# Layer 0: the up projections made ahead of the sweep become plain fp32 products, 50 of them in place of 46

## The chip, the cores and the metric

The kernel runs on one core of one Trainium2 chip, in one launch. The metric is the time of the launch on the device in microseconds (us). Five engines work side by side, each through its own queue of instructions in a fixed order: PE (TensorE, matrix products), DVE (VectorE), ACT (ScalarE), POOL (GpSimd) and SP (SyncE, which here only starts transfers). An instruction waits at the head of its queue until what it reads is there and what it overwrites is free, and everything behind it on that engine waits too.

## The reference

Two layers of a diffusion transformer over 256 latent tokens and 256 context tokens of width 1024. Each layer mixes tokens (a convolution and two kinds of attention), and then a feed-forward with very many small experts follows. Only that last part is touched:

```python
def chunk_step(xc):
    q = (xc @ w_q).reshape(PEER_CHUNK, PEER_HEADS, 2, PEER_D_KEY)
    s = jnp.einsum('chpk,hpnk->chpn', q, sub_keys).astype(jnp.float32)
    top_s, top_i = lax.top_k(s, PEER_TOPK)
    ...
    best_s, best_pos = lax.top_k(cand_s.reshape(PEER_CHUNK, PEER_HEADS, n_cand), PEER_TOPK)
    idx = jnp.take_along_axis(...)
    g = jax.nn.softmax(best_s, axis=-1).astype(xc.dtype)
    act = jax.nn.gelu(jnp.einsum('cd,chkd->chk', xc, jnp.take(u, idx, axis=0)))
    return jnp.einsum('chk,chkd->cd', g * act, jnp.take(v, idx, axis=0))
```

There are 16,384 rows in `u` and in `v`. For each token 8 heads choose 16 rows each by a score; the token's product with a chosen row of `u` goes through gelu and is the weight of the same row of `v`. Layer 0 does this for all 512 tokens (four tiles of 128), layer 1 for the 256 latent ones.

## The kernel before

**Dense and gathered tiles.** In layer 0 three of the four tiles of 128 tokens are treated densely (384 tokens, `nd`): every row of `u` is multiplied with every token, and a matrix of gates (zero for rows that were not chosen) is multiplied in behind the gelu. The fourth tile is treated by gathers: POOL fetches the chosen rows (tiles `gru` and `grv`), and DVE takes the products. The 16,384 rows are cut into 128 blocks of 128, which the code calls `e`; in this text a block is called an expert.

**The up projection of an expert** (`act`, L622 ff.) multiplies a block of `u` (1024 x 128, eight chunks of 128) with the 384 tokens. The operands are split: `hi` is the value rounded to a narrower fp32 (fp32r), `lo` the rest, and each chunk is three products, hi·hi, lo·hi and hi·lo (`mm3`, L118 to L121), so 24 products of 128x384 into the PSUM tile `psu`. The tokens' halves are `h2` (tiles `ahi_m`, `alo_m`). The block of `u` is split for each expert: ACT makes `hi_u` (L97); `lo_u` is made by POOL in four pieces (L104) for the experts that are made ahead, and by DVE in one (L99) for the others. ACT then takes the gelu into `gact` (L632).

**Ahead of the sweep.** 46 experts have their up projection made ahead: the first `GA[0]` = 4 stay in SBUF, the next `SPILL[0]` = 42 are written to DRAM (`spilled`) and read back later (`gback`). This fills PE while the routing goes on: 16 query projections (`psq`, split as above), the choice of the best 16 by DVE (L644 to L648), then for each of the 24 groups of 16 tokens four DVE operations on 128x2048 f16 (`ohA`, `ohB`, `ohC`, L782 to L786), 32 small PE products (`psg`, L792), four ACT copies (`stage`, L794) and one write of 1 MB of gates to DRAM (`gd`).

**The sweep** (`sweep`) goes through all 128 experts: gelu times gate (`gr`, read back from `gd` for eight experts at a time), a split into `whi` and `wlo`, and the down projection, 18 products of 128x512 into the PSUM tiles `acc`. For an expert that was not made ahead, its up projection comes in between. Gathers are started between experts; `ahead` = `GA[l] + SPILL[l]` is in the formula that paces them.

**Order.** The code says what is to be done; a scheduler that keeps its own timeline decides the order on each engine when the program is built, so an edit in one place can move rows elsewhere. Tiles of one tag share buffers: `raw_u` has three, `hi_u` and `lo_u` have two each, `psu` has two.

**Layer 1** has the same structure with 192 tokens, and its up projections are plain fp32 products already (L630): eight matmuls per expert straight from `raw_u` and the unsplit tokens `h2raw`. In the trace each of these stands as two instructions, so 16 per expert.

## Time and profile before

| | before |
|---|---|
| time, median of 3 runs | 2625.38 us (2622.39 to 2629.26) |
| profiled execution, its own time | 2625.23 us |
| span of its trace, first to last instruction | 2623.5 us |
| PE busy | 2490.8 us, 95% of the span |
| DVE / ACT / POOL busy | 1828.0 / 1054.5 / 1048.3 us |
| mean granted TensorE clock | 0.981 |

Busy times of PE count from the start of a product to its modelled end, and products overlap, so a busy PE can still be starting fewer products than it could. The rate at which it starts them is read from the distance between starts in the timeline. All times in the trace are counted from the start of the span.

### The profile page before, as it was taken

The numbers are of one execution on the slowest core, as the hardware profiler recorded it, in microseconds if no ns is written. First come the engines' busy times: TensorE is split into PE (matmuls) and PEld (weight loads), VectorE is DVE, ScalarE is ACT, GpSimd is POOL, SyncE is SP. The second block draws the span as 40 slices with busy tenths as digits, with TensorE's granted clock in tenths as the row PEclk, the third lists the DMA queues.
The fourth block names the chain that finished last, engine by engine and source line by source line (L and its number), as shares of the span: only waits on it lengthen the run. The fifth ranks groups of instructions, "written<-read, shape, count | busy, mean of one in ns | idle before, by whom it ended". The sixth has DMA issues, their size and how long they took to land.

```text
span 2623.5 us, 38317 instructions
## 1 busy us (share of the span) xinstructions
PE 2490.8 (95%) x13837; PEld 2018.2 (77%) x13837; DVE 1828.0 (70%) x3506; ACT 1054.5 (40%) x1710; POOL 1048.3 (40%) x967
## 2 busy tenths in 40 slices
PE   7999999888899999999999998998999999999997
PEld 4755788777798888998999987856997656777774
DVE  1754589999546678887888885474994457666667
ACT  3345633367533333333333334455454333323333
POOL 4713434768542245544445441831500114332222
PEclk9999999999999999999999999998999999999999
DMA  7343364366878889999999992541579879999996
GB/s 270 115 158 123 131 243 150 116 220 256 298 256 286 289 294 360 334 339 325 357 332 343 339 327 77 195 133 40 166 254 352 281 264 339 381 344 363 352 364 221
DMA packets 274223, 681.44 MB, mean 260 GB/s; under 512 B 25024, under 2 KB 129008, under 8 KB 270960
## 3 DMA queue, kind: packets, MB, share of 16 engines
q1 hardware_dynamic: 127040, 423.48, 45.4%
q0 software_dynamic: 55296, 201.35, 20.7%
q10 hardware_dynamic: 91696, 54.15, 7.2%
q8 instruction: 109, 1.79, 0.3%
q14 instruction: 82, 0.67, 0.1%
HBM read 628.63 MB, written 49.44 MB: 258 GB/s over the span
## 4 chain that ended last, share of the span: by engine, by line
PE 63%; DVE 13%; issue 7%; DMA 7%; POOL 3%; ACT 2%; ACTq 0%; DVEq 0%; SPq 0%; POOLq 0%
PE psu L630 11%; PE acc L119 6%; PE acc L120 6%; PE acc L121 6%; PE acc L834 4%; PE psu L121 4%; PE psu L119 4%; PE psu L120 4%; DMA grv<-in_v,eidx 2%; POOL gru L918 2%; DMA gr<-gd 2%; PE psada L221 2%; DVE ohC L786 1%; DVE ohB L783 1%; PE psq L119 1%
## 5 line engine op out<-in xcount | busy, mean ns | idle before, releaser
L120 PE MATMUL acc<-lo_v,whi 128*128 128x512 f32 x1024 | 410.1, 401 | 1.2 <-DVE lo_v L99 1.0
L99 DVE TENSOR_TENSOR lo_v<-raw_v,hi_v 128x1024 fp32r<-128x1024 f32 x256 | 312.0, 1222 | 137.8 <-ACT hi_v L97 137.2
L97 ACT ACTIVATE hi_v<-raw_v 128x1024 fp32r<-128x1024 f32 x256 | 268.7, 1053 | 274.7 <-PE acc L121 232.1
L630 PE MATMUL psu<-h2raw,raw_u 128*128 128x192 f32 x2048 | 365.4, 330 | 11.5 <-DMA raw_u<-in_u 7.7
L121 PE MATMUL acc<-hi_v,wlo 128*128 128x512 f32 x1024 | 373.1, 392 | 0.0
L630 PEld LDWEIGHTS psu<-h2raw,raw_u 128*128 128x128 f32 x2048 | 339.4, 191 | 42.8 <-issue 21.8
L119 PE MATMUL psu<-ahi_m,hi_u 128*128 128x384 f32 x1024 | 348.5, 340 | 10.4 <-ACT gact L632 10.4
L121 PE MATMUL psu<-ahi_m,lo_u 128*128 128x384 f32 x1024 | 349.3, 341 | 4.9 <-DVE lo_u L99 2.9
L119 PE MATMUL acc<-hi_v,whi 128*128 128x512 f32 x1024 | 346.7, 404 | 4.4 <-ACT hi_v L97 3.5
L120 PE MATMUL psu<-alo_m,hi_u 128*128 128x384 f32 x1024 | 348.4, 340 | 0.0
L918 POOL DMA_INDIRECT gru<-in_u_rows,eidx x128 | 184.8, 1444 | 274.6 <-DVE gback L819 142.0
L119 PEld LDWEIGHTS acc<-hi_v,whi 128*128 128x128 f32 x1024 | 184.8, 188 | 105.4 <-ACT gact L632 32.5
L913 DVE SCALAR_TENSOR_TENSOR h2n<-grv,dots,h2n 128x1024 f32<-128x1024 f32 x190 | 242.9, 1279 | 25.0 <-DMA grv<-in_v,eidx 24.0
L104 POOL TENSOR_TENSOR lo_u<-raw_u,hi_u 128x256 fp32r<-128x256 f32 x184 | 209.8, 1172 | 104.7 <-ACT hi_u L97 97.9
L906 DVE SCALAR_TENSOR_TENSOR gru<-gru,h2n 128x1024 f32<-128x1024 f32 x192 | 232.4, 1220 | 25.0 <-DMA gru<-in_u_rows,eidx 23.2
L918 POOL DMA_INDIRECT grv<-in_v,eidx x128 | 171.9, 1343 | 187.0 <-DVE h2n L913 160.7
L918 POOL DMA_INDIRECT gru<-in_u_rows,egl x64 | 91.0, 1422 | 376.8 <-DMA spilled<-gact 125.6
L120 PEld LDWEIGHTS acc<-lo_v,whi 128*128 128x128 f32 x1024 | 192.7, 188 | 55.8 <-DVE lo_v L99 8.2
L121 PEld LDWEIGHTS acc<-hi_v,wlo 128*128 128x128 f32 x1024 | 192.4, 188 | 37.0 <-DVE wlo L824 0.3
L119 PEld LDWEIGHTS psu<-ahi_m,hi_u 128*128 128x128 f32 x1024 | 194.4, 190 | 16.2 <-ACT gact L632 11.7
L121 PEld LDWEIGHTS psu<-ahi_m,lo_u 128*128 128x128 f32 x1024 | 194.4, 190 | 10.2 <-DVE lo_u L99 3.9
L120 PEld LDWEIGHTS psu<-alo_m,hi_u 128*128 128x128 f32 x1024 | 194.6, 190 | 4.1
(286 smaller groups left out, 4468.1 us busy)
## 6 DMA issues: line engine op xcount, KB each, us to landing
raw_u<-in_u SPq DMA_DIRECT2D x256, 512.0 KB, 6.0
raw_v<-in_v SPq DMA_DIRECT2D x256, 512.0 KB, 6.4
ada<-in_ada SPq DMA_DIRECT2D x96, 512.0 KB, 5.6
gd<-stage SPq DMA_DIRECT2D x24, 1024.0 KB, 5.8
gr<-gd ACTq DMA_DIRECT2D x16, 1536.0 KB, 21.5
raw_wq<-in_w_q SPq DMA_DIRECT2D x32, 512.0 KB, 3.7
raw_wout<-in_w_out SPq DMA_DIRECT2D x24, 512.0 KB, 3.5
gd<-stage SPq DMA_DIRECT2D x12, 960.0 KB, 5.0
```

Source lines behind the costliest of these rows:

```text
L97: S.activation(hi, raw, AF.Copy)
L99: V.tensor_tensor(lo, raw, hi.bitcast(F32), ALU.subtract)
L104: hold(lo_eng.tensor_tensor(lo[sl], raw[sl], hi[sl].bitcast(F32), ALU.subtract), after)
L119: return [PE.matmul(o, lhsT=ahi, rhs=bhi, start=first, stop=False), PE.matmul(o, lhsT=ahi, rhs=blo, start=False, stop=False), PE.matmul(o, ...
L120: PE.matmul(o, lhsT=ahi, rhs=blo, start=False, stop=False),
L121: PE.matmul(o, lhsT=alo, rhs=bhi, start=False, stop=last)]
L221: PE.matmul(ps[o:o + 32, :], lhsT=scw[:, c, :], rhs=w[:, q, :], start=c == 0, stop=c == NC - 1)
L630: PE.matmul(ps[:, :nd], lhsT=u[:, c, :], rhs=h2raw[:, c, :nd], start=c == 0, stop=c == NC - 1)
L834: return [PE.matmul(acc[1][0][k * H:(k + 1) * H], lhsT=ga[:, P:P + H], rhs=raw[:, k * 512:(k + 1) * 512], start=e == 0, stop=e == NE - 1) ...
L906: return V.scalar_tensor_tensor(r, r, 1.0, h2n[g], op0=ALU.mult, op1=ALU.mult, accum_out=dots[:, s:s + 1])
L913: return V.scalar_tensor_tensor(h2n[g], r, dots[:, s:s + 1], h2n[g], op0=ALU.mult, op1=ALU.add)
L918: d = G.indirect_dma_start(out=r, out_offset=None, in_=a["v_rows" if k >= ns else "u_rows"], in_offset=bass.IndirectOffsetOnAxis(ap=eidx[g ...
```

## The change

All experts ahead of the sweep in layer 0 are multiplied as layer 1 does it: plain fp32, straight from `raw_u`, with no split of `u`. There are now 50 of them (`SPILL[0]` = 46). The unsplit tokens that this needs are made on POOL as `h2[0] + h2[1]`, one addition of 128x384 per chunk, into a new tile `hr`. The other 78 experts keep the split and DVE's `lo_u`.

```diff
-SPILL = {0: 42, 1: 32}
+SPILL = {0: 46, 1: 32}
...
+        hr = None
+
         def act(e, tag="gact", bufs=GA[l]):
             ps = bank("mm", f"psu{l}_{e}")
-            if first:
+            if first and e >= GA[l] + SPILL[l]:
                 u = piece(a["u"][l, e], TP, "u", f"u{l}_{e}", G if e < GA[l] + SPILL[l] else V)
                 gemm_t(ps[:, :nd], u, h2, slice(0, nd))
             else:
                 u = load(a["u"][l, e], TP, "u", f"u{l}_{e}")
                 for c in range(NC):
-                    PE.matmul(ps[:, :nd], lhsT=u[:, c, :], rhs=h2raw[:, c, :nd], start=c == 0, stop=c == NC - 1)
+                    PE.matmul(ps[:, :nd], lhsT=u[:, c, :], rhs=hr[:, c, :nd], start=c == 0, stop=c == NC - 1)
...
+            hr = rt.tile([P, NC, nd], F32, name=f"hr{l}") if first else h2raw
...
             for h in range(8):
+                if first:
+
+                    G.tensor_tensor(hr[:, h, :], h2[0][:, h, :nd].bitcast(F32), h2[1][:, h, :nd].bitcast(F32), ALU.add)
```

The built programs show where this puts the instructions. On POOL, in the norm ahead of the queries, `alo_m` is the low half of the tokens that the query products read, and `lo_wq` that of their weights. Before:

```order
L196 TENSOR_TENSOR alo_m0_877<-hraw_g010_2590,ahi_m0_876 128x256
L196 TENSOR_TENSOR alo_m0_877<-hraw_g012_2610,ahi_m0_876 128x256
L196 TENSOR_TENSOR alo_m0_877<-hraw_g014_2630,ahi_m0_876 128x256
L196 TENSOR_TENSOR alo_m0_877<-hraw_g016_2650,ahi_m0_876 128x256
L104 TENSOR_TENSOR lo_wq02_2910<-raw_wq02_2907,hi_wq02_2909 128x256 x4
```

And now:

```order
L196 TENSOR_TENSOR alo_m0_877<-hraw_g010_2590,ahi_m0_876 128x256
L657 TENSOR_TENSOR hr0_2673<-ahi_m0_876,alo_m0_877 128x384 x2
L196 TENSOR_TENSOR alo_m0_877<-hraw_g012_2610,ahi_m0_876 128x256
L196 TENSOR_TENSOR alo_m0_877<-hraw_g014_2630,ahi_m0_876 128x256
L657 TENSOR_TENSOR hr0_2673<-ahi_m0_876,alo_m0_877 128x384 x4
L196 TENSOR_TENSOR alo_m0_877<-hraw_g016_2650,ahi_m0_876 128x256
L657 TENSOR_TENSOR hr0_2673<-ahi_m0_876,alo_m0_877 128x384 x2
L104 TENSOR_TENSOR lo_wq02_2682<-raw_wq02_2679,hi_wq02_2681 128x256 x4
```

All eight additions stand between these rows, six of them ahead of the last `alo_m`.

On PE, the place is the start of the sweep: the last up projections ahead of the first `acc`. Before, the first `acc` stands behind expert 38, and experts 39 to 45 follow between the `acc`:

```order
L119 MATMUL psu0_38_7278<-ahi_m0_876,hi_u0_38_7281 128x384
L120 MATMUL psu0_38_7278<-alo_m0_877,hi_u0_38_7281 128x384
L121 MATMUL psu0_38_7278<-ahi_m0_876,lo_u0_38_7282 128x384
L119 MATMUL acc000_7579<-hi_v0_0_7595,whi0_0_7589 128x512
L120 MATMUL acc000_7579<-lo_v0_0_7596,whi0_0_7589 128x512
```

Now all 50 plain products and two split experts (50 and 51) stand ahead of it:

```order
L632 MATMUL psu0_48_6553<-hr0_2673,raw_u0_48_6554 128x384 x8
L632 MATMUL psu0_49_6567<-hr0_2673,raw_u0_49_6568 128x384 x8
...
L119 MATMUL psu0_51_8325<-ahi_m0_876,hi_u0_51_8328 128x384
L120 MATMUL psu0_51_8325<-alo_m0_877,hi_u0_51_8328 128x384
L121 MATMUL psu0_51_8325<-ahi_m0_876,lo_u0_51_8329 128x384
L119 MATMUL acc000_6586<-hi_v0_0_6602,whi0_0_6596 128x512
```

Of the plain products, 32 experts and a half stand ahead of the last `psg` of the routing and 17 and a half behind it; before it was 33 experts and 20 products, and 12 experts.

On ACT, whose queue also starts the reads of `gr` and `gback`, the place is the first read of gates. Before, it stands behind the gelu of expert 34:

```order
L97 ACTIVATE hi_u0_36_7207<-raw_u0_36_7205 128x1024
L632 ACTIVATE gact0_34_7164<-psu0_34_7130 128x384
L97 ACTIVATE hi_u0_37_7244<-raw_u0_37_7242 128x1024
L817 DMA gr0_0_7586<-gd0_2571 128x24x128
L711 DMA gback0_4_7708<-spilled0_6019 128x384
```

Now it stands behind the gelu of the last expert ahead, number 49, and behind two splits that wait for their loads:

```order
L97 ACTIVATE hi_u0_50_8263<-raw_u0_50_8261 128x1024
L634 ACTIVATE gact0_48_6564<-psu0_48_6553 128x384
L97 ACTIVATE hi_u0_51_8328<-raw_u0_51_8326 128x1024
L634 ACTIVATE gact0_49_6578<-psu0_49_6567 128x384
L823 DMA gr0_0_6593<-gd0_2571 128x24x128
L717 DMA gback0_4_6715<-spilled0_5936 128x384
```

## Rows read from the trace of the kernel before

**Rows 1.** The profile page, its first part: busy us of each engine, its share of the span and its instructions.

```profile
PE 2490.8 (95%) x13837; PEld 2018.2 (77%) x13837; DVE 1828.0 (70%) x3506; ACT 1054.5 (40%) x1710; POOL 1048.3 (40%) x967
```

**Rows 2.** Busy time by stretch: the stretch, its length, then for each engine its busy us and (x) its instructions, the granted clock, the DMA share and GB/s. The first stretch goes from the first `psu` of layer 0 to the first `acc` of the sweep, the next two are its parts up to the last `psg` and behind it, the fourth is the sweep up to its last `acc`, the last a piece of the sweep.

```profile
446.45:715.90 269.45, 224.72 (x1730) 211.17 (x1726) 230.24 (x318) 156.39 (x197) 186.32 (x153) 0.96 0.61 217
446.45:684.60 238.15, 201.05 (x1611) 188.70 (x1608) 227.72 (x314) 145.73 (x183) 174.60 (x136) 0.96 0.57 203
684.60:715.90 31.30, 23.67 (x121) 22.47 (x120) 2.52 (x5) 10.66 (x15) 11.72 (x17) 0.89 0.98 324
715.90:1621.40 905.50, 901.07 (x4441) 803.16 (x4441) 684.86 (x857) 320.07 (x443) 377.11 (x284) 1.00 0.88 308
1000.00:1400.00 400.00, 397.43 (x2010) 360.63 (x2009) 330.02 (x418) 141.37 (x193) 192.55 (x144) 1.00 0.96 339
```

**Rows 3.** The same stretches, PE's instructions on `psu` alone: busy us, (x) products, clock, DMA.

```profile
446.45:715.90 269.45, 181.75 (x936) 0.96 0.61 217
715.90:1621.40 905.50, 397.64 (x2136) 1.00 0.88 308
```

**Rows 4.** The first stretch, PE's instructions on `psg` alone.

```profile
446.45:715.90 269.45, 54.03 (x768) 0.96 0.61 217
```

**Rows 5.** The sweep, PE's instructions on `acc` alone.

```profile
715.90:1621.40 905.50, 553.40 (x2304) 1.00 0.88 308
```

**Rows 6.** Timeline of PE: start, us, instruction, count. Two split up projections of 384 tokens in a row, two down projections of 512 columns in a row, 56 instructions of plain fp32 of 192 columns in layer 1 as one row, two `psg`, and eight instructions of plain fp32 of 128 columns as one row.

```profile
446.73 0.34 PE L120 MATMUL psu<-alo_m,hi_u 128*128 128x384 f32 x1
446.90 0.34 PE L121 MATMUL psu<-ahi_m,lo_u 128*128 128x384 f32 x1
...
1102.36 0.39 PE L121 MATMUL acc<-hi_v,wlo 128*128 128x512 f32 x1
1102.59 0.39 PE L119 MATMUL acc<-hi_v,whi 128*128 128x512 f32 x1
...
1915.71 9.27 PE L630 MATMUL psu<-h2raw,raw_u 128*128 128x192 f32 x56
...
682.04 0.22 PE L792 MATMUL psg<-ohA,ohB 128*128 128x128 f16 x1
682.10 0.22 PE L792 MATMUL psg<-ohC,ohB 128*128 128x128 f16 x1
...
450.37 1.05 PE L668 MATMUL pssc<-key,q 128*128 128x128 f32 x8
```

**Rows 7.** PE's waits in the first stretch: engine and line that waited, for what, us in total, times, the longest.

```profile
PE psrt L767 <- DVE ij L757: 12.6, 4, 7.3
PE psg L792 <- DVE ohC L786: 12.3, 13, 2.2
PE psu L119 <- ACT gact L632: 9.1, 3, 6.2
PE psg L792 <- DVE ohA L786: 7.7, 6, 1.5
```

**Rows 8.** One of DVE's four costliest groups from 446 to 684 us (layer 0), and the same operation from 1930 to 2000 us (layer 1, POOL idle): count, busy us, mean ns.

```profile
L782 DVE TENSOR_TENSOR ohA<-sT,iota_t 128x2048 f16<-128x2048 f16 x24 | 38.2, 1594 | 6.2 <-PE psg L792 6.2
...
L782 DVE TENSOR_TENSOR ohA<-sT,iota_t 128x2048 f16<-128x2048 f16 x10 | 12.2, 1222 | 6.9 <-PE psg L792 6.8
```

**Rows 9.** Timeline of POOL around 560 us, with the idle time ahead of the instruction in brackets, and of DVE: two operations while POOL had nothing to do, and two while it had.

```profile
559.71 9.12 POOL L104 TENSOR_TENSOR lo_u<-raw_u,hi_u 128x256 fp32r<-128x256 f32 x8 [9.56 <-ACT hi_u L97]
572.71 6.05 POOL L104 TENSOR_TENSOR lo_u<-raw_u,hi_u 128x256 fp32r<-128x256 f32 x4 [3.88 <-ACT hi_u L97]
...
569.64 1.23 DVE L782 TENSOR_TENSOR ohA<-sT,iota_t 128x2048 f16<-128x2048 f16 x1 [6.21 <-PE psg L792]
574.74 1.76 DVE L782 TENSOR_TENSOR ohA<-sT,iota_t 128x2048 f16<-128x2048 f16 x1
```

**Rows 10.** Timeline of ACT's queue of transfers, DVE and PE at the start of the sweep: the first read of gates is issued, the first product of gelu and gate that waits for it, the first `whi`, the first `acc`.

```profile
694.17 0.59 ACTq L817 DMA_DIRECT2D gr<-gd  x1
707.78 1.03 DVE L819 TENSOR_TENSOR gact<-gact,gr 128x384 f32<-128x384 f32 x2 [18.44 <-DMA gback<-spilled]
715.33 0.92 ACT L823 ACTIVATE whi<-gact 128x384 fp32r<-128x384 f32 x2
715.88 0.51 PE L119 MATMUL acc<-hi_v,whi 128*128 128x512 f32 x1 [0.70 <-ACT whi L823]
```

**Rows 11.** The chain of work that ended last, its piece for that first read of gates: start, us.

```profile
694.17 13.29 DMA gr<-gd
```

**Rows 12.** From issue to landing of a transfer, least, median and most, first for `raw_u`, then for `gr`.

```profile
DMA to landing us min/median/max: 3.4/6.0/14.5
...
DMA to landing us min/median/max: 7.7/18.6/29.9
```

**Rows 13.** Timeline of POOL and PE ahead of the third query projection: the last `alo_m`, the first `lo_wq` behind them, and the last query product of the first pair with the wait behind it.

```profile
329.16 0.74 POOL L196 TENSOR_TENSOR alo_m<-hraw_g,ahi_m 128x256 fp32r<-128x256 f32 x1 [1.20 <-ACT ahi_m L195]
333.44 2.10 POOL L104 TENSOR_TENSOR lo_wq<-raw_wq,hi_wq 128x256 fp32r<-128x256 f32 x3 [3.54 <-ACT hi_wq L97]
...
332.29 0.28 PE L121 MATMUL psq<-ahi_m,lo_wq 128*128 128x256 f32 x1
333.84 1.16 PE L668 MATMUL pssc<-key,q 128*128 128x128 f32 x8 [1.28 <-ACT q L664]
```

**Rows 14.** Busy time by stretch as in rows 2, from the fourth query projection to the first `psu`.

```profile
349.00:446.45 97.45, 97.45 (x807) 85.80 (x805) 91.83 (x612) 27.73 (x39) 35.26 (x49) 1.00 0.54 184
```

## Prediction

> **What bounds the kernel now.** I read the page first: PE is busy for 95% of the span [rows 1], so the question is where PE has time to spare. The times by stretch answer it [rows 2]. In the sweep, from 715.9 to 1621.4 us, PE is busy for 901 of 905.5 us. In the 269.45 us ahead of it, from the first `psu` to the first `acc`, PE shows 225 us and DVE 230 us; up to the last `psg` DVE is busy for 227.7 of 238.15 us, so there DVE sets the pace and PE waits.
>
> Busy PE time says too little, because products overlap. The starts in the timeline say more [rows 6]: a split product of 384 columns starts 0.173 us behind the one before it, a down projection of 512 columns 0.2275 us (0.23 as printed), a `psg` 0.056 us. With the counts [rows 3 to 5]:
>
> Ahead of the sweep: 936 x 0.1734 = 162.3, 768 x 0.056 = 43.0, some 25 other products at 0.11 = 2.8, together 208.1 us of 269.45. **PE stands idle for 61.3 us there.** The waits say why [rows 7]: 32.6 us for DVE's `ij` and one-hots, 9.1 us for ACT behind the late gates, the rest too short to be listed. The granted clock was 0.96 there and 1.00 in the sweep [rows 2]; what that cost is inside the 61.3.
>
> In the sweep: 2136 x 0.1734 + 2304 x 0.2275 = 370.4 + 524.2 = 894.6 of 905.5 us, so 10.9 us idle. The sweep is a wall of PE work: it shortens only by products taken out of it.
>
> **The change, step by step.**
>
> *The price of a plain product.* Layer 1 has them with 192 columns: 56 instructions from 1915.71 us in 9.27 us, the last ending some 0.33 us behind its start, so (9.27 - 0.33)/55 = 0.1625 us each [rows 6]. With 128 columns, eight take 1.05 us, (1.05 - 0.275)/7 = 0.111 us. For 384 columns twice the 192 gives 0.325; the line through both points gives 0.1625 + 192 x 0.0515/64 = 0.317. I take 0.322, near twice the longer row. An expert has 16: 5.15 us (5.07 to 5.20), against 24 x 0.1734 = 4.16 us split. So each of the 50 experts costs PE 0.99 us more, the four taken out of the sweep included, since they cost 4.16 there: **+49.5 us** of PE work (+45.5 to +52).
>
> The Trainium skill, "FP8 and Floating Point Precision", section "TensorE Precision Notes", says that a true fp32 product takes four passes through the array. The rows agree that plain is dearer than three split products; that rule alone, at four thirds of 4.16 us, would give 5.55 us for an expert and +69 us.
>
> *The idle time that this can use.* A plain product waits for its load and for a free PSUM tile, no more for ACT's and POOL's split. POOL loses 184 pieces of `lo_u`, and that frees DVE: the one-hot of 128x2048 took 1.594 us on average in layer 0 and 1.222 in layer 1, where POOL did nothing [rows 8]; one after the other, 1.23 us while POOL had just nothing to do and 1.76 while it had [rows 9]. Four such operations for 24 groups: 96 x 0.37 = 36 us less for DVE, apart from what stands ahead of them. So DVE no longer sets the pace. PE has 32.5 experts ahead of the last `psg`, 32.5 x 5.15 + 43.0 + 2.8 = 213 us against the 238 of before, while DVE comes down from 228 to some 190. PE waits little then; I leave 5 us idle up to the last plain product (0 to 15; of the 61.3 us, 61.3 - 32.6 - 9.1 = 19.6 were too short to be listed, and not all of them need be DVE's).
>
> The Trainium skill, "SBUF — State Buffer", section "Who interferes with whom", says that a VectorE operation with two inputs in SBUF and a GpSimd one that reads SBUF shut each other out for the whole of an instruction. The trace agrees with its 1.23 and 1.76 us.
>
> *The start of the sweep.* Before, the first gates were asked for at 694.17 us, landed 13.29 us later, and `acc` began at 715.88 [rows 10, 11]. Now ACT asks for them behind the gelu of expert 49. From the last plain product: a gelu, 0.5 us, or up to a load of `raw_u` more, 6.0 us, since `hi_u` of expert 51 stands ahead on ACT; 7.7 us at least for the gates, 13.3 as before [rows 12]; some 1.5 us for gate, `whi` and `acc`. That is 10 to 21 us. PE has experts 50 and 51 for it, 8.3 us, so it idles 2 to 12.5 us; I take **8 us**, a little over the middle. Of the 61.3 us idle before, 5 + 8 stay.
>
> *The additions on POOL.* `alo_m` on POOL takes 0.74 us for 256 columns [rows 13], so `hr` about 1.1. Six of the eight stand ahead of the last `alo_m`, which the query products need: 6.6 us of POOL work, minus its idle time of 2 us there, so that piece comes some 4.5 us later, and `lo_wq` behind it as well. PE had 1.5 us without a product there (332.29 to 333.84), and modulation products of layer 1 can fill some more. I take **+3 us** (0 to +5), carried by PE to the first `psu`, since from 349 us up to there PE is busy all the time [rows 14].
>
> *What costs nothing.* Four more writes and reads of 192 KB lie under plain products, where DMA was busy to 0.61 [rows 2]. ACT and DVE lose work in the sweep, where PE sets the pace. Gathers go 4% faster per step (39 instead of 35 of 259 steps by the end of the experts ahead, then 3.14 for 3.03 per expert); where both experts' blocks are read, DMA is at 0.96 already [rows 2], so this cover is thin. If it is gone, the 10.9 us idle of the sweep grow, by perhaps 5 us. Layer 1 keeps its work; its rows are shuffled a little.
>
> **Sum.** 49.5 - 61.3 + 5 + 8 + 3 = +4.2 us. Against the profiled execution, 2625.23 (the median of the runs shown is 2625.38, the same): **2629.5 us**. PE's work grows by almost what it had idle; the 61.3 us are used up and not gained. The same by times: first `psu` at 449.5, last plain product at 758 (257.5 + 43.0 + 2.8 + 5 behind it), first `acc` at 774, then 76 x 4.16 + 524.2 + 10.9 = 851, last `acc` at 1625 for 1621.4.
>
> **The rivals.** A measurement here can tell about 0.3%, 7.9 us, from no change.
>
> A, *nothing waits any more* (faster). DVE set the pace, it is 36 us faster, and gates and POOL's additions are hidden as well: 49.5 - 61.3 = -11.8, 2613.4 us. For it speaks that 61 us idle is much. Against it: the gates are asked for with 8.3 us of cover and never landed in under 7.7. It decides in favour of faster where less than 3.9 us remain of the 16 that I leave. That DVE is 36 us faster does not decide it, since PE's own 213 us are next, 25 us under the 238. The Trainium skill, "SBUF — State Buffer", section "Who interferes with whom", stands behind this rival: by it DVE is rid of POOL altogether.
>
> B, *the sweep waits for its gates* (slower). The place is the first `gr`: behind a late load of `raw_u` (6.0 us) it takes 18.6 us, as its median in the sweep, because eleven other reads follow at once: 6 + 18.6 + 1.5 - 8.3 = 17.8 us idle for my 8, 2639 us. For it speaks ACT's new order. Against it: before the sweep few other transfers are under way. It decides from a wait of 11.7 us.
>
> C, *the plain products wait for their loads* (slower). A `raw_u` is held through the product now, so with three buffers a load has two products, 10.3 us, to land. Its median is 6.0, its most 14.5 [rows 12]. At 14.5, an expert would take (14.5 + 5.15)/3 = 6.55 us; over the 32 that share the time with 1 MB writes, +45 us, 2670. It decides from 10.5 us to landing. Layer 1 works this way with half as long a product, which speaks against it.
>
> **How the numbers follow.** Forecast 0.52 (own range 2621 to 2637, a little of it above the bound), A 0.14, B 0.25, C 0.09. Faster is A, 0.14; slower is B, C and 4 in 100 of the forecast, 0.38; the rest, 0.48, is within 0.3%. The range reaches into A and through B: 2616 to 2645.
>
> **What would show it.** Right: plain instructions of 384 columns at 0.32 us from start to start; the one-hots at 1.22 us; PE near 100% from 450 to 758 us with DVE under 90%; one wait of PE for `whi` at some 765 us; the first `acc` at 770 to 780, 55 us later than before, and the last at 1620 to 1632. Wrong: waits of PE for `raw_u`; a `psu` that starts at more than 0.33 us; DVE still above 1.5 us for a one-hot; a sweep with more than 16 us idle.

## The result, and the profile after

The changed kernel took 2648.14 us (median of 7 runs, 2637.91 to 2656.93) beside 2625.38 for the kernel before: ratio 1.0081, 95% interval 1.0066 to 1.0096. It is 17 to 25 us slower. The forecast was 2629.5 with a range up to 2645: wrong, by 3 us beyond the range. Single executions of one kernel on one chip lie up to 1.1% apart (the kernel before on one of the chips: 2617.03 to 2645.75 us), so below the ratios tell how fast a kernel is, and a profile, which is one execution, only where its time lies.

The first row of the page after [rows 1]: PE is busy for 43 us more, POOL for 209 us less.

```profile
PE 2533.7 (96%) x13437; PEld 1960.3 (74%) x13437; DVE 1767.6 (67%) x3502; ACT 1003.0 (38%) x1656; POOL 839.7 (32%) x791
```

Busy time by stretch, columns as in [rows 2]. The cuts: first `psu`, last `psg`, first `acc`, last `acc` of layer 0, first `psq` of layer 1, end.

```profile
449.90:664.70 214.80, 214.80 (x1313) 142.40 (x1310) 172.15 (x311) 113.01 (x147) 0.00 (x0) 1.00 0.63 216
664.70:775.90 111.20, 98.92 (x333) 61.50 (x330) 5.17 (x6) 15.73 (x28) 0.00 (x0) 0.95 0.61 201
775.90:1634.70 858.80, 848.31 (x4128) 749.68 (x4129) 674.87 (x851) 302.72 (x417) 356.84 (x256) 1.00 0.90 315
1634.70:1847.60 212.90, 192.96 (x1017) 132.70 (x1015) 113.49 (x233) 102.26 (x202) 89.80 (x116) 0.93 0.36 122
1847.60:2647.50 799.90, 763.29 (x4193) 577.00 (x4191) 531.16 (x1103) 286.22 (x510) 208.19 (x189) 0.99 0.85 302
```

Of the kernel before, the two stretches behind the last `acc` of layer 0, which the prediction had not cut:

```profile
1621.20:1825.80 204.60, 187.70 (x1017) 129.64 (x1015) 114.92 (x233) 105.38 (x202) 96.71 (x116) 0.94 0.38 127
1825.80:2623.50 797.70, 762.20 (x4193) 576.44 (x4191) 529.60 (x1104) 288.48 (x513) 208.32 (x189) 0.98 0.85 303
```

Stretch by stretch, forecast and profile:

| | forecast | profile after | off by |
|---|---|---|---|
| first `psu` | 449.5 | 449.9 | +0.4 |
| from there to the first `acc` | 324.5 | 326.0 | +1.5 |
| sweep, first to last `acc` | 851 | 858.8 | +7.8 |
| last `acc` to the end | 1002.3 | 1012.8 | +10.5 |

The part that the prediction worked out at length came within 2 us. The 18 us beyond it lie where its sum had nothing: in the sweep, in which the diff alters only what follows from `SPILL` (which experts stand ahead, and the pace of the gathers), and in layer 1, in which it alters nothing.

### The profile page after: what moved, and what is told of

The parts are those of the page before. It is cut to its first block, busy times and chain, and to the rows that moved or that the text cites. A ratio compares the mean times of both kernels' runs of the same rounds, so it can differ in the third digit from the quotient of the medians.

```text
span 2647.5 us, 37240 instructions
## 1 busy us (share of the span) xinstructions
PE 2533.7 (96%) x13437; PEld 1960.3 (74%) x13437; DVE 1767.6 (67%) x3502; ACT 1003.0 (38%) x1656; POOL 839.7 (32%) x791
## 5 line engine op out<-in xcount | busy, mean ns | idle before, releaser
L99 DVE TENSOR_TENSOR lo_v<-raw_v,hi_v 128x1024 fp32r<-128x1024 f32 x256 | 312.1, 1222 | 124.8 <-ACT hi_v L97 123.8
L119 PE MATMUL acc<-hi_v,whi 128*128 128x512 f32 x1024 | 341.3, 405 | 20.5 <-ACT whi L829 13.0
L632 PE MATMUL psu<-hr,raw_u 128*128 128x384 f32 x800 | 265.6, 489 | 0.0
L634 ACT ACTIVATE gact<-psu 128x384 f32<-128x384 f32 (+1 forms) x256 | 104.4, 408 | 343.8 <-PE psu L632 293.3
L632 PEld LDWEIGHTS psu<-hr,raw_u 128*128 128x128 f32 x800 | 148.7, 190 | 98.5 <-issue 3.6
L121 PE MATMUL psu<-ahi_m,lo_u 128*128 128x384 f32 x624 | 210.4, 337 | 3.4 <-DVE lo_u L99 3.3
L119 PE MATMUL psu<-ahi_m,hi_u 128*128 128x384 f32 x624 | 210.3, 337 | 1.3 <-ACT gact L634 1.3
L120 PE MATMUL psu<-alo_m,hi_u 128*128 128x384 f32 x624 | 209.9, 336 | 0.0
L829 ACT ACTIVATE whi<-gact 128x128 fp32r<-128x128 f32 (+1 forms) x178 | 72.5, 408 | 290.1 <-PE acc L120 146.4
```

Source lines behind the costliest of these rows:

```text
L99: V.tensor_tensor(lo, raw, hi.bitcast(F32), ALU.subtract)
L119: return [PE.matmul(o, lhsT=ahi, rhs=bhi, start=first, stop=False), PE.matmul(o, lhsT=ahi, rhs=blo, start=False, stop=False), PE.matmul(o, ...
L120: PE.matmul(o, lhsT=ahi, rhs=blo, start=False, stop=False),
L121: PE.matmul(o, lhsT=alo, rhs=bhi, start=False, stop=last)]
L632: PE.matmul(ps[:, :nd], lhsT=u[:, c, :], rhs=hr[:, c, :nd], start=c == 0, stop=c == NC - 1)
L634: S.activation(ga[:, :nd], ps[:, :nd], AF.Gelu_apprx_tanh)
```

## Experiments

Each is the changed kernel with the edit shown, unless its text says "the kernel before". The time is the median, the ratio that to runs of the kernel before on the same chip, with its 95% interval.

### A. Is it the plain products, or the order that their count brings?

**split50**

```
-SPILL = {0: 42, 1: 32}        # kernel before
+SPILL = {0: 46, 1: 32}
```

> The kernel before with 50 experts ahead of the sweep instead of 46, all of them split products as before; no plain product and no sum on POOL. Its layer 1 comes out of the scheduler in nearly the order of the changed kernel (11 differing places on PE, against 107 to the kernel before). Theory 'order': the 10.4 us that layer 1 lost come from the order of its instructions, which the count of experts ahead moves, and not from the plain products; then layer 1, from the last acc of layer 0 to the end, takes 1010 to 1015 us here too, layer 0 ends within 5 us of 1621, and the kernel takes about 2634 us. Rival 'clock': PE without pauses ahead of the sweep is what makes the granted clock lower in layer 1; then layer 1 stays at 1002 us, since PE waits for DVE here as before, and the kernel takes 2625 us.

2642.07 us, ratio 1.0045 (1.0025 to 1.0065). More than half of the loss comes without a single plain product. In its profile, the shortest of its nine executions, the stretch up to layer 1's `psq` took 210.2 us against 204.6, while layer 0 ended at 1618.5. All of layer 1 took 1007.2 us: more than the 1002 of "clock" and less than the 1010 to 1015 of "order". "Clock" does not fit, since PE waited for DVE here as before; for "order" the test is split50_order below.

**plain46** and **plain38**

```
-SPILL = {0: 46, 1: 32}
+SPILL = {0: 42, 1: 32}        # plain38: 34
```

> The changed kernel with 46 experts ahead in place of 50, all plain. By the price of 0.99 us for each plain expert layer 0 ends 4 us earlier, at about 1631 us. Layer 1's order on POOL is that of the changed kernel word for word, on PE it is nearer to the kernel before (65 differing places with 271 rows) than to the changed one (50 places with 1055 rows). If POOL's order sets layer 1, it takes 1012 us and the kernel 2643; if the order on PE and ACT sets it, 1002 to 1006 us and the kernel 2633 to 2637. Rival 'clock': 1012 us, as in the changed kernel, since PE has no pauses here either.

> The changed kernel with 38 experts ahead in place of 50, all plain. By 0.99 us for each plain expert that does not fill idle time of PE, layer 0 ends 12 us earlier, at 1623 us, as long as the experts behind the last psg (about 5 of them, 26 us) still cover the write of the last group and the read of the first gates: first acc at about 714 us (12 experts at 5.16 us earlier). Rival: the last groups land later than that; then PE waits 10 to 20 us longer for the gates and the gain is gone, layer 0 ends at 1633 or later. Layer 1, whose order is nearer to the kernel before on PE (51 places, 303 rows): 1002 to 1006 us if the order on PE sets it, 1012 us if POOL's does. Kernel: 2625 to 2635 us.

plain46: 2641.09 us, 1.0046 (1.0027 to 1.0064); layer 0 ended at 1633.4, `psq` 212.4 us behind it. plain38: 2637.4 us, 1.0036 (1.0021 to 1.0051); layer 0 ended at 1621.2, first `acc` at 713.3, `psq` 215.4 us behind the end. From 50 to 38 experts layer 0 lost 13.5 us (12 expected), the ratio 0.45%: the price of 0.99 us for an expert fits here. In the two pairs below that differ by the same twelve experts, the ratio falls by 0.19 and 0.21%, some 5 us.

On layer 1 the two do not decide. plain38 took 1014.4 us there, as POOL's order would have it, but plain46 1005.6, which was the forecast for PE's and ACT's: its stretch up to `psq` is long, the rest (793.2 us) short, and that rest lies between 789 and 804 us over all kernels here. In the stretch itself the trace of plain46 has the changed kernel's order on PE, DVE, ACT and POOL, so it cannot tell PE's order from POOL's.

### B. Layer 1: the place of one weight split

POOL around 1700 us in the changed kernel, in the kernel before and in order1: the start, us, and in each case the split of the last w_in_n piece, `lo_win`, among those of w_in_t, `lo_wint` (four instructions each).

```profile
1695.83 5.95 POOL L104 TENSOR_TENSOR lo_wint<-raw_wint,hi_wint 128x256 fp32r<-128x256 f32 x8
1701.73 2.78 POOL L104 TENSOR_TENSOR lo_win<-raw_win,hi_win 128x256 fp32r<-128x256 f32 x4
```

```profile
1681.21 3.64 POOL L104 TENSOR_TENSOR lo_wint<-raw_wint,hi_wint 128x256 fp32r<-128x256 f32 x4
1684.82 2.84 POOL L104 TENSOR_TENSOR lo_win<-raw_win,hi_win 128x256 fp32r<-128x256 f32 x4
1687.62 2.84 POOL L104 TENSOR_TENSOR lo_wint<-raw_wint,hi_wint 128x256 fp32r<-128x256 f32 x4
```

```profile
1690.13 3.19 POOL L109 TENSOR_TENSOR lo_wint<-raw_wint,hi_wint 128x256 fp32r<-128x256 f32 x4
1693.28 2.83 POOL L109 TENSOR_TENSOR lo_win<-raw_win,hi_win 128x256 fp32r<-128x256 f32 x4
1697.31 3.37 POOL L109 TENSOR_TENSOR lo_wint<-raw_wint,hi_wint 128x256 fp32r<-128x256 f32 x4
```

The scheduler of the changed kernel put two `lo_wint` ahead of `lo_win`. PE, changed kernel, at that place:

```profile
1703.19 0.50 PE L120 MATMUL pszn<-lo_win,ahi_h 128*128 128x512 f32 x1 [1.96 <-POOL lo_win L104]
...
1704.24 0.63 PE L120 MATMUL pszn<-lo_win,ahi_h 128*128 128x512 f32 x1
1704.66 0.63 PE L121 MATMUL pszn<-hi_win,alo_h 128*128 128x512 f32 x1
```

PE waits 1.96 us, and a microsecond later eight products start 0.41 to 0.43 us apart, where 0.23 is usual for 512 columns [rows 6]. In gback_sp (section C) the trace has the same order of instructions in this stretch on PE, DVE, ACT and POOL, and the same wait, but the products behind it start 0.23 us apart:

```profile
1694.16 0.50 PE L120 MATMUL pszn<-lo_win,ahi_h 128*128 128x512 f32 x1 [2.01 <-POOL lo_win L104]
```

The 10 us at this place by stretch, first of the changed kernel, then of gback_sp:

```profile
1700.80:1710.80 10.00, 8.04 (x34) 6.24 (x33) 4.99 (x13) 2.50 (x6) 4.94 (x7) 0.83 0.76 258
```

```profile
1691.80:1701.80 10.00, 7.99 (x47) 6.69 (x46) 5.00 (x13) 2.83 (x6) 4.93 (x7) 1.00 0.88 310
```

The granted clock was 0.83 against 1.00: the slow products ran at the lower level, 1.2 GHz in place of 2.4. The twenty products from the wait to the next `psgt` took 6.31 us, in gback_sp 4.77. So the wait cost 2 us, and where the clock fell another 1.5. It fell at this place in plain46 and plain38 too (waits of 1.96 and 3.60 us), and not in split50 (1.64 us). The two together are less than half of the 8.3 us by which the stretch is longer than before; the rest lies mostly behind this place and was not taken apart.

**order1** (`win_made` holds the last w_in_n split's two instructions; `behind` is passed through `piece` to `split`)

```
+        made[0] = S.activation(hi, raw, AF.Copy)
+        if behind:
+            hold(made[0], behind[0])
+            after = behind[1]
...
-            w = piece(a["w_in_t"][l, j], TP, "u", f"wint{l}{j}", G)
+            w = piece(a["w_in_t"][l, j], TP, "u", f"wint{l}{j}", G, behind=win_made if l and j == 7 else None)
```

> The changed kernel with one more dependency in layer 1 alone: the second of two weight splits of w_in_t that ran on POOL and ACT ahead of the last split of w_in_n now runs behind it, as in the kernel before. Theory 'order': the wait of 2.0 us for lo_win and the slower products behind it at 1703 us go, and the stretch from the last acc of layer 0 to layer 1's first psq falls from 213 us to 205 to 209 (it was 204.6 before, and 210 to 215.5 in the four other kernels, all of which had the later lo_win); the kernel gains 4 to 8 us, 2640 to 2644. Rival: the stretch is long for the other differences of order (61 places on ACT, 110 on PE); then it stays at 211 to 213 and the time at 2648.

2637.56 us, 1.0057 (1.0036 to 1.0078); the stretch is 203.9 us for 212.9. "Order" holds for the stretch. The ratio fell by 0.24%, which is just within what the two intervals leave open (0.26%). Nor is it the place of one split alone that changed: with the new dependency the scheduler put 31 other places of this stretch on PE into another order.

**split50_order**: the kernel before with 50 split experts and the same edit.

> The kernel before with 50 split experts ahead, as split50 (ratio 1.0045), and the last w_in_n split ahead in layer 1. Theory 'order': split50's loss comes from layer 1's order, so the stretch up to psq falls from 210.2 to 204 to 207 us and the kernel takes 4 to 8 us less than split50, a ratio of 1.0015 to 1.003. If the order were all of the loss, the ratio would be 1.000. Rival: split50 is slow for another reason that its profile did not show; then the ratio stays at 1.004 or more.

2628.05 us, 1.0007 (0.9989 to 1.0026): split50's whole loss is gone, 0.38%, more than the two intervals leave open (0.27%). Its stretch: 204.7 us.

Over all kernels here: in the five with `lo_win` behind (the changed kernel, split50, plain46, plain38, gback_sp), the stretch took 210.2 to 215.4 us, and PE waited 1.6 to 3.6 us for `lo_win`; in the fifteen with it ahead, 203.6 to 206.7, with waits of at most 0.5 us. In the kernel before and in four others the scheduler had put it there without an edit (gr_pool, gr_pool_hr, glag5, gb6 below); these four have ratios of 1.0044 to 1.0067 where the changed kernel has 1.0081.

### C. The start of the sweep: ACT's queue

In the first stretch of the changed kernel PE waited once, for 12.3 us at the first `acc`; the waits of before [rows 7] are gone. PE's waits from 449 to 777 us, then ACT with its queue of transfers from 755 us on:

```profile
PE acc L119 <- ACT whi L829: 12.3, 1, 12.3
```

```profile
755.42 0.59 ACTq L823 DMA_DIRECT2D gr<-gd  x1
756.04 4.99 ACTq L717 DMA_DIRECT2D gback<-spilled  x1
756.18 0.47 ACT L634 ACTIVATE gact<-psu 128x384 f32<-128x384 f32 x1
761.06 6.59 ACTq L717 DMA_DIRECT2D gback<-spilled  x4
767.69 0.53 ACTq L823 DMA_DIRECT2D gr<-gd  x1
768.91 5.33 ACTq L717 DMA_DIRECT2D gback<-spilled  x3
774.34 1.06 ACT L97 ACTIVATE hi_u<-raw_u 128x1024 fp32r<-128x1024 f32 x1 [17.68 <-issue]
775.30 0.51 ACT L829 ACTIVATE whi<-gact 128x384 fp32r<-128x384 f32 x1
```

The first product of gelu and gate began at 766.28 us, so the gates were there; ACT reached `whi` nine microseconds later, since the issues of `gback` stand ahead of it in its program and hold it. An issue, the time in which an engine's queue starts a transfer, usually takes 0.33 us. Those of `gback` in layer 0 that take 2 to 8 us, seven with 33.2 us in all, are each the first `gback` behind a `gr`. Before there were six with 32.5 us. What such an issue waits for, no run shows.

**gback_sp**

```
-            nc.scalar.dma_start(ga[:, :nd], spilled[:, e - GA[l], :])
+            nc.sync.dma_start(ga[:, :nd], spilled[:, e - GA[l], :])
```

> The changed kernel with the reads of spilled activations (gback) issued on SP's queue instead of ACT's. Theory: the wait of 12.3 us at the start of the sweep is ACT held in the issues of reads that stand ahead of whi in its program, not the landing of the gates; the gate multiply was done at 766.3 us and whi ran at 775.3. Then the wait falls to about 4 us, the first acc is at 767 to 769 us and the kernel 8 us faster, 2640 us, with layer 1 unchanged in length (its order differs in 20 places from the changed kernel's). Rival: the gates land late themselves; then the wait stays within 2 us of 12.3, or moves to the gate multiply.

2628.07 us, 0.9994 (0.9980 to 1.0008): 20 us less by the medians, more than twice what was expected. PE's wait in the first stretch:

```profile
PE acc L119 <- ACT whi L829: 3.3, 1, 3.3
```

The first `acc` came at 766.9 us. That is 9 us; of the rest, 6.6 us lie in layer 1's sweep (612.9 us from first `acc` to end for 619.5), whose `gback` reads the edit moves too. Layer 1's sweep took 609.2 to 615.9 us in the eight profiles with `gback` on SP and 615.5 to 627.5 in the twelve with it on ACT. Long issues on ACT are not the whole of that, since in the changed kernel they come to 2.2 us there (1.46 and 0.75); the rest stays open.

**gbsp_order** and **before_gbsp_order** (the second: the kernel before)

> The changed kernel with both: gback reads on SP's queue, and the last split of w_in_n ahead in layer 1. If the two effects are separate, gback_sp's 2628 falls by what the order alone gives, to 2620 to 2624; if gback on SP had already taken the order's loss away, it stays at 2628. Layer 0 ends at 1626 to 1627 as in gback_sp.

> The kernel before with the same two edits and nothing of the change: gback reads on SP and the w_in_n split ahead in layer 1 (without that edit, gback on SP brings the later lo_win into the kernel before too). It gives the price of the change without both side effects. Theory: ACT is held in six gback issues before as well (32.5 us in all), but PE waits for whi only 0.9 us in its sweep, so layer 0 gains at most the few us between the last split psu and the first acc; 2620 to 2628 us, and the change itself then costs -2 to +4 us, as its sum without the sweep and layer 1 says (+3.4 + 50 - 47.4 - 8). Rival: SP's queue is what helps, in layer 1's sweep too, and the kernel before gains the 20 us that the changed one did: 2608 us, and the change costs what it did, some 20 us.

gbsp_order: 2622.16 us, 0.9991 (0.9977 to 1.0005). By the ratio that is only 0.03% below gback_sp, although the stretch is 5 us shorter (205.4 for 210.4): with `gback` on SP the time does not show the order's gain. That speaks for the second case of the expectation, but 5 us are 0.2%, which the two intervals leave open. before_gbsp_order: 2625.13 us, 0.9990 (0.9977 to 1.0003). With both side effects out, the two kernels cannot be told apart: the change itself costs nothing, to within some 0.2%. The sum, +4.2 us less the 9 us of wait that `gback` on SP took away, would be -5 us, at the edge of that. Why the same move of `gback` gives the kernel before nothing stays open; there the profile, one of its longer executions, had 12 us less in layer 1's sweep, but 10 us more ahead of the first `psu`.

**p38_gbsp_order**

> 38 experts ahead, all plain, with gback reads on SP and the w_in_n split ahead in layer 1; its layer 1 has word for word the order of the kernel before with the same two edits. By 0.99 us for each plain expert beyond those that fill idle time, 12 fewer than 50 give -12 us in layer 0 against gback_sp's 1626.7, as long as the gates' wait does not grow by more than the 4 us that it has left: layer 0 ends at 1615 to 1619 and the kernel takes 2610 to 2618 us. Rival: the gates of the last groups decide, the first acc stays at 713 us as in plain38, and gback on SP gives nothing here: layer 0 ends at 1621, the kernel takes 2622 us.

2618.55 us, 0.9972 (0.9961 to 0.9982), just above the 2610 to 2618 of the expectation. The first `acc` came at 710.0 us, 7.5 us of PE's time still waiting for `whi`, now because the gates themselves were late.

### D. What keeps the first gates back

**gr_pool**, **gr_pool_hr** and **p38_gr_pool**

```
-            hr = rt.tile([P, NC, nd], F32, name=f"hr{l}") if first else h2raw
+            hr = es.enter_context(tc.tile_pool(name=f"hrp{l}", bufs=1)).tile(...) if first else h2raw
...
-                nc.scalar.dma_start(gr, gd[1][:, :, e:e + EG, :])
+                (G if l == 0 and e == 0 else nc.scalar).dma_start(gr, gd[1][:, :, e:e + EG, :])
```

(gr_pool_hr without the first line's change; p38_gr_pool with both, 38 experts, `gback` on SP and order1's edit)

> The changed kernel with the first read of the gates issued on POOL's queue, where nothing else waits, and with hr moved to the top of the memory, since in the changed kernel the tile of the first gates lies where hr lies (hr is read up to the last plain product). Then the first gates can be asked for as soon as the last group has been written, some 90 us ahead of the first acc. What is left of the wait at the start of the sweep is ACT alone: one issue of gback held behind the second gates' read (4.4 us in the changed kernel). Theory: first acc at 763 to 768 us instead of 775.9, layer 0 8 to 12 us shorter. Its layer 1 has, without any edit there, the last w_in_n split ahead again, so its stretch up to psq should be 204 to 207 us. Kernel: 2630 to 2636 us. Rival: the gates' landing never was the wait; then the first acc stays at 775.

> The same without moving hr: the first gates on POOL's queue, into a tile that shares its place with hr. If the place is what makes the gates late, they are asked for only behind the last plain product, as in the changed kernel, and land some 10 to 13 us later, at 766 to 768 us; the first acc then at 768 to 772 us. If the place does not matter, the first acc is where gr_pool has it. Its layer 1 too has the last w_in_n split ahead: 204 to 207 us up to psq.

> 38 experts ahead, all plain, gback reads on SP, the first gates on POOL's queue with hr out of their way, the w_in_n split ahead in layer 1. Against p38_gbsp_order, whose PE waited 7.5 us for the gates with its first acc at 710.0 us: the gates are there by then, so the first acc comes at 702 to 704 us and the kernel takes 6 to 8 us less, 2611 to 2613 us for 2618.6. Rival: SP, held by gback's issues at that place (15.8 us for seven), delays raw_u or raw_v next, and half of the gain is lost: 2615.

2642.6 us, 1.0067 (1.0048 to 1.0087); 2642.12 us, 1.0065 (1.0046 to 1.0084); 2626.75 us, 1.0002 (0.9990 to 1.0015). First `acc` at 780.7, 779.3 and 710.4 us. All three missed. POOL in gr_pool:

```profile
757.58 1.67 POOL L823 DMA_DIRECT2D gr<-gd  x1 [318.52 <-DMA raw_u<-in_u]
```

POOL had nothing to do for 318 us and still issued the read only behind the last plain product. So neither ACT's order nor the address of `hr`, which the first line of the edit moves, was what held it. What was left: `hr` lives in a pool that closes with the routing, and the sweep's pool is opened in that space; its first tiles wait for the pool's last reader.

**hr_out** and its control **gb6** (gb6: the second edit alone)

```
-            hr = rt.tile([P, NC, nd], F32, name=f"hr{l}") if first else h2raw
+            hr = gapool.tile([P, NC, nd], F32, name=f"hr{l}") if first else h2raw
...
-            ga = sw.tile([P, nd], F32, tag="gback", name=f"gback{l}_{e}", bufs=GB)
+            ga = sw.tile([P, nd], F32, tag="gback", name=f"gback{l}_{e}", bufs=6 if l == 0 else GB)
```

(hr_out with order1's edit)

> The changed kernel with hr in the layer's own memory pool instead of the routing's, six buffers for gback in layer 0 in place of eight (to make the room), and the w_in_n split ahead in layer 1 as in order1, with which it is compared. Theory 'pool': in the changed kernel the sweep's memory is that of the routing, hr among it, so the first gates cannot be read before the last plain product; with hr outside, the read of the first gates moves ahead of the gelu of expert 34 on ACT, and the first acc comes among the plain products, at 690 to 705 us in place of 775. The idle time of 14 us at the start of the sweep goes, less some us for ACT held by gback issues with gelus behind them; layer 0 ends at 1618 to 1624 (order1: 1630), the kernel takes 2626 to 2632 us (order1: 2637.6). Rival: the gates' read stands elsewhere (on ACT behind gelus, whatever the memory); then no acc before 770 and 2637 us.

> The changed kernel with six buffers for gback in layer 0 in place of eight and nothing else; the control for hr_out. Its layer 1 has by itself the last w_in_n split ahead. If the buffers do nothing, it is as order1: first acc at 775 us, layer 0's end at 1630 to 1635, 204 to 207 us up to layer 1's psq, 2636 to 2643 us. If fewer buffers keep ACT's queue freer, the first acc comes some us earlier.

gb6: 2636.93 us, 1.0055 (1.0029 to 1.0081), first `acc` at 776.9: as order1 (1.0057, 775.0), so the buffers do nothing. hr_out: 2636.46 us, 1.0037 (1.0015 to 1.0058). The first gates were asked for at 682.30 us in place of 755.42, and the first `acc` came at 707.0, among the plain products. "Pool" is right on that; the gain in time was missed (0.20% below order1, with layer 0 ending at 1640.0 in a profile that was the longest of nine executions). ACT in hr_out, and PE's wait from 449 to 800 us:

```profile
682.30 0.59 ACTq L830 DMA_DIRECT2D gr<-gd  x1
682.93 8.01 ACTq L724 DMA_DIRECT2D gback<-spilled  x5
690.98 0.53 ACTq L830 DMA_DIRECT2D gr<-gd  x1
693.12 5.55 ACTq L724 DMA_DIRECT2D gback<-spilled  x1
698.77 0.49 ACT L641 ACTIVATE gact<-psu 128x384 f32<-128x384 f32 x1 [18.62 <-issue]
```

```profile
PE psu L639 <- ACT gact L641: 9.4, 1, 9.4
```

The same held ACT now has gelus behind it, and PE waits for a PSUM tile instead of for `whi`.

**hr_out_gbsp**, **p38_hr_out**, **p32_hr_out** (hr_out with `gback` on SP and 50, 38 and 32 experts ahead)

> hr_out with gback reads on SP's queue, beside gbsp_order (2622 us, first acc at 771.6). With ACT free of long issues and the first gates read early, PE has neither wait: of gbsp_order's 7 to 9 us idle at the start of the sweep nearly all goes, 2612 to 2617 us. Then the changed kernel would be faster than the kernel before by 0.3 to 0.5%. Rival: SP, with gback reads that wait for their spilled writes, holds raw_u and raw_v loads now that both kinds run side by side; PE then waits for raw_u or raw_v some 5 to 10 us, and nothing is gained over 2622.

> hr_out_gbsp with 38 experts ahead in place of 50. Each plain expert costs PE 0.99 us more than a split one, and none of the last twelve fills idle time any longer: -12 us against hr_out_gbsp by that price, as long as the gates come early; against p38_gbsp_order (2618.6, of which 7.5 us wait for the gates) -5 to -8 us: 2604 to 2612 us. Rival: with fewer plain products PE runs out of work before the last groups are written, and it takes as long as p38_gbsp_order.

> p38_hr_out (ratio 0.9943) with 32 experts ahead, all plain. They end with the last psg at about 664 us, and the first gates land 24 us behind it (688 us for the first acc in p38_hr_out). If PE fills that time with the split products of the first experts made in the sweep (two PSUM tiles, 8.3 us), it idles some 15 us there, for 6 us saved by six fewer plain products: ratio 0.997 to 0.998. If those products, not being bound to their acc, fill more of it, 0.992 to 0.994.

hr_out_gbsp: 2615.73 us, 0.9964 (0.9948 to 0.9979). ACT's queue and PE's wait there:

```profile
674.38 8.34 ACTq L830 DMA_DIRECT2D gr<-gd  x2
```

```profile
PE psu L639 <- ACT gact L641: 1.5, 1, 1.5
```

First `acc` at 688.3 us, 1.5 us of waiting left of 12.3. p38_hr_out: 2611.15 us, **0.9943 (0.9924 to 0.9963), faster than both kernels**. p32_hr_out: 2630.98 us, 1.0014 (1.0001 to 1.0027), a miss beyond both expectations. Its PE ran out of work ahead of the first `acc`:

```profile
PE acc L125 <- ACT whi L836: 19.4, 1, 19.4
```

In all three the first `acc` comes 25 to 26.5 us behind the last `psg`, whatever PE has to do meanwhile: experts ahead pay as far as they fill that time, and by the price above cost 0.99 us each beyond it. That is not all of the miss: by its products, PE also idles 28.5 us inside the sweep of p32_hr_out and 13.5 in that of p38_hr_out, and why is open.

### E. The sweep

By its products (1824 x 0.1734 + 2304 x 0.2275 = 840.4 us) the sweep of the changed kernel idles 18.4 us, for 10.9 before. PE's waits from 776 to 1634.7 us (of the first row, 12.3 us are the wait at the first `acc`, shown above), then those of the kernel before:

```profile
PE acc L119 <- ACT whi L829: 13.0, 2, 12.3
PE psu L121 <- DVE lo_u L99: 3.3, 2, 2.1
PE acc L119 <- ACT hi_v L97: 3.1, 2, 2.0
PE acc L120 <- DVE lo_v L99: 2.0, 2, 1.7
```

```profile
PE psu L121 <- DVE lo_u L99: 2.9, 3, 1.6
PE psu L119 <- ACT gact L632: 1.2, 1, 1.2
PE acc L119 <- ACT whi L823: 0.9, 2, 0.7
```

Some 1.6 us of the growth are the clock: behind the wait of 12.3 us it was granted at the lower level up to 779.2 us, and eight products start 0.43 us apart there. Behind the waits two causes can be seen. ACT at 911 us, and then PE: `gback` behind a `gr` again, with `whi` and `hi_v` behind it. Last, DVE at 1500 us: it stands in front of a gathered row, with `lo_v` behind it.

```profile
911.27 0.53 ACTq L823 DMA_DIRECT2D gr<-gd  x1
...
914.76 7.63 ACTq L717 DMA_DIRECT2D gback<-spilled  x1
922.43 0.52 ACT L829 ACTIVATE whi<-gback 128x384 fp32r<-128x384 f32 x1 [7.34 <-PE acc L121]
```

```profile
923.96 0.50 PE L119 MATMUL acc<-hi_v,whi 128*128 128x512 f32 x1 [2.00 <-ACT hi_v L97]
```

```profile
1506.22 1.28 DVE L919 SCALAR_TENSOR_TENSOR h2n<-grv,dots,h2n 128x1024 f32<-128x1024 f32 x1 [6.43 <-DMA grv<-in_v,eidx]
1507.42 0.55 DVE L830 TENSOR_TENSOR wlo<-gact,whi 128x384 fp32r<-128x384 f32 x1
1507.89 2.35 DVE L99 TENSOR_TENSOR lo_v<-raw_v,hi_v 128x1024 fp32r<-128x1024 f32 x2
```

**glag5**

```
-GLAG = 3
+GLAG = 5
```

> The changed kernel with two more buffers for gathered rows (GLAG 5 in place of 3), so that DVE uses a row two steps later than it did. Theory for the sweep's idle time, which rose from 10.9 to 18.5 us: DVE stands in front of a gather that has not landed (6.4 us at 1500), with a split for PE behind it; with two more rows under way these waits go, and the time that PE loses inside the sweep falls to 11 to 14 us; what remains is ACT held by gback issues (3.1 us). Rival: it stays at 18 or more. Layer 1 here has the last w_in_n split ahead: 204 to 207 us up to psq. Kernel 2630 to 2638 us.

2637.67 us, 1.0044 (1.0029 to 1.0060). The idle time inside the sweep is 11.8 us, and of PE's waits there one row is left, ACT's:

```profile
PE acc L119 <- ACT hi_v L97: 3.7, 2, 2.5
```

This fits the gathers as a cause. It does not settle the size, since this idle time also scatters between executions and orders: 13 to 15 us in five of the other kernels with 50 plain experts, 17 to 22 in three, 8 to 13 with split ones. In the time it gave nothing clear: the ratio is 0.13% below order1's, and layer 1's sweep, whose buffers `GLAG` sets as well, took 627.5 us, the longest here. Nor is it known why the split kernels, split50 with the same pace of gathers among them, have less of it.

## Why the prediction was wrong, step by step

- **The price of a plain product: right.** Six of them in a row in the changed kernel:

```profile
689.62 2.10 PE L632 MATMUL psu<-hr,raw_u 128*128 128x384 f32 x6
```

  With the last one ending 0.49 us behind its start, (2.10 - 0.49)/5 = 0.322 us, as taken; some 5.16 us for an expert. By the four passes of a true fp32 product that the Trainium skill states, "FP8 and Floating Point Precision", section "TensorE Precision Notes", the prediction's estimate was 5.55; the measurement decides.
- **DVE no longer sets the pace: right.** The one-hot of 1.59 us [rows 8] takes 1.22, and DVE waits for PE's `psg`. The group from 440 to 780 us, and what DVE waited for ahead of it, 30.8 us in all:

```profile
L788 DVE TENSOR_TENSOR ohA<-sT,iota_t 128x2048 f16<-128x2048 f16 x24 | 29.3, 1224 | 30.8 <-PE psg L798 30.8
```

  The Trainium skill, "SBUF — State Buffer", section "Who interferes with whom", says that a VectorE instruction with two inputs in SBUF contends with a GpSimd one that reads SBUF. The trace agrees: POOL had no instruction between 449.9 and 775.9 us, by the stretches above, and the one-hot is back at the 1.22 us of layer 1 [rows 8].
- **The additions on POOL: the delay right, its way to PE smaller, and the +3.4 us at the first `psu` for +3 in part luck.** The first `alo_m` of this norm on POOL already came 2.0 us later than before (214.45 us for 212.41), 113 us ahead of the first addition (327.65). The last `alo_m` came 6.3 us later (335.43 for 329.16), so the additions held it for 4.2 us, with 4.5 worked out; of these, 1.4 reached the first `psu`. Two profiles without the additions, before_gbsp_order and split50_order, began at 456.0 and 454.9.
- **The start of the sweep: right in sum, by another way and so by luck.** Idle 13.9 us (326.0 less 312.1 of products) for 5 + 8. PE lost 1.6 us, not 5, up to the last plain product, and 12.3 instead of 8 behind it. The step put this down to the gates' landing; ACT, held in the issues of `gback`, came 9 us behind the gates. That the gates were asked for so late at all was said to follow from ACT's order; the runs showed the pool of `hr` (hr_out).
- **"If it is gone, the 10.9 us idle of the sweep grow, by perhaps 5 us": a step that was set at nothing in the sum.** They grew by 7.5, to 18.4, past the 16 us that it gave as a sign of being wrong. This step and the next took the time out of the range.
- **"Layer 1 keeps its work; its rows are shuffled a little": the step that failed most.** The work is the same, and the shuffle of its rows cost 10.5 us in the profile, 8.3 of them up to `psq`, where PE waited for a weight split that had moved behind another on POOL; order1 took 9 us of the stretch back. In the time, the order was worth 0.24% with plain products (some 6 us, not clear of the noise by itself), 0.38% with split ones, and 0.03% with `gback` on SP. The shuffle was seen and not priced.
- **Rivals.** A's condition, that gates are hidden as well, came true only in hr_out_gbsp, which took 2615.73 us for A's 2613.4. B named the right place; the wait of 12.3 us is past its 11.7, but what waited was ACT. C did not come: no wait of PE for `raw_u` ahead of the sweep. (Its 2670 us add the 45 us to the kernel before; added to the forecast they give 2674.)

By the ratios, the way from the changed kernel to the fastest: layer 1's order -0.24% (order1), `gback` off ACT's queue -0.66% (gbsp_order), `hr` out of the routing's pool -0.27% (hr_out_gbsp), 38 experts in place of 50 -0.21% (p38_hr_out). The shares depend on the sequence: with `gback` first they are -0.87% for it (gback_sp) and -0.03% for the order behind it. The intervals leave some 0.2 to 0.3% open at each step.

## What to carry to other kernels

Where a scheduler places the instructions, a change in one layer reorders the others: compare the order of the untouched part as well, engine by engine, and price each place where an operand that PE reads has moved behind other work on its engine. A new buffer in a pool that is handed over makes the next phase wait for its last reader; where a tile lives is part of the change. And a transfer issued on a computing engine's queue can hold that engine, so what stands behind an issue in its program belongs on the path.

## What the runs showed of the hardware

- In layer 0, a `gback` issued on ACT's queue as the first transfer behind a `gr` read (1.5 MB), within 5 us of it, took 1.0 to 9.2 us to issue over all profiles, for a median of 0.33 us of the others, and ACT ran nothing of what stood behind it. In split50 and split50_order one came 14 to 15 us behind its `gr` and took 0.33 us. On SP, no `gback` issue took 2 us; but where `gback` was on SP, a second `gr` issued on ACT right behind the first took 4.4 to 9.1 us.
- One and the same wait of PE, 1.96 us in the changed kernel and 2.01 in gback_sp, with the same order of instructions around it, was followed once by eight products at the lower clock, 0.41 to 0.43 us from start to start, and once by products at 0.23.
- A plain fp32 instruction of 384 columns starts 0.322 us behind the one before it, 16 for an expert, against 24 of 0.173 us for the split.
